# Hi and lo parts of the latent tokens and FFN rows in one tile, and one 512-column matmul of the hi weights with both

## The chip, the cores and the metric

One core of a Trainium2 chip. The metric is the device time of one execution in microseconds: before, the median of three runs is 1982.09 us (1978.47 to 1982.77).

## What is computed

One layer of a hybrid backbone on a latent stream `x` and a context stream `ctx` of 256 tokens each, with 2048 features:

```
px = modulate(rms_norm(x, norm_mix), sh1, sc1) @ w_in          # and pc, from ctx
yx = concat(rwkv(px), short_conv(px), fourier(px)) @ w_out     # the scans of x start from ctx's last states
x  = x + ga1 * yx
h  = modulate(rms_norm(x, norm_ffn), sh2, sc2)
x  = x + ga2 * ((silu(h @ w_gate) * (h @ w_up)) @ w_down)      # 5632 hidden features
out = rms_norm(x, norm_final)
```

All weights and inputs are float32.

## The kernel before

Features lie on the 128 partitions, so 2048 features are 16 **K-tiles**, and the 256 tokens are the columns that a matmul streams. The large products are made in three matmuls of a faster type (`float32r`): a value is split into a hi part, its rounding to that type, and a lo part, the rest. A K-tile of `w^T x` is then hi weights times hi tokens, hi weights times lo tokens, and lo weights times hi tokens, all added in one PSUM bank:

```python
    def mm3(self, out, wh, wl, xh, xl, start, stop):
        self.mm(out, wh, xh, start, False)
        self.mm(out, wh, xl, False, False)
        self.mm(out, wl, xh, False, stop)
```

Every call of `mm` (line 233, so the trace shows line 233 for all matmuls) is a load of 128 x 128 weights and a matmul of 256 columns. `wblock` (L271) brings weights: a DMA from SP's queue into `w`, a cast to `whi` (L266), and a subtraction into `wlo` (L269); each of the three has three places. `XH1` and `XL1` are the hi and lo parts of the latent tokens, `XH0` and `XL0` those of the context.

The stages, in the order of time:
- **Phase A and keys** (to about 280 us): norms, modulation vectors, first projections, for both streams (`mm6`, six matmuls a K-tile).
- **The recurrence** (to about 1150 us): chunked scans of eight pairs of heads for both streams. PE's order is written by hand (`manual_schedule`): between the small matmuls of the scans stand "filling products", a K-tile or a few at a time (`fillers`, `project_steps`). Those of the values take both streams; 26 blocks of 128 columns take the latent alone: 8 queries (`query`), 2 gates, 12 of the short convolution, 4 of the Fourier mixing. Their bank is read by `conv3`, by copies or by multiplications. Then come the products with `w_out` (`out_proj`).
- **SwiGLU, gate and up** (1180 to 1717 us): 44 rows of 128 hidden features. A row has four blocks of weights of 8 K-tiles each (gate, up, gate, up), and two banks, `gu0` and `gu1`. The first two rows go side by side before the norm's factor is known; the 42 others run one after another. ACT takes silu of `gu0` (L1165), DVE multiplies by `gu1` (L1166), and the row is split into `HH` and `HL`. In four rows `modvec` (L1082) brings 16 pieces of `wmb` through two places on SP's queue and adds them up on DVE (L1093).
- **SwiGLU, down** (1717 to 1965 us): 16 blocks of 128 output features, each 44 K-tiles in six blocks of weights (the last one half as long) into a bank `dn`, which DVE scales and adds to `X1` (L1183); then the final norm.

In the SwiGLU stage the casts to `whi` are ACT's, and of the subtractions every third is POOL's and the others DVE's. On all engines but PE in the recurrence a scheduler sets the order when the program is built, from a timeline of its own.

Of the kernel before, what the change touches and what calls it, by code (L numbers as in the profile page):

```python
# [10 lines left out]
F32 = mybir.dt.float32  # L11
F32R = mybir.dt.float32r
# [5 lines left out]
P = 128  # L18
D = 2048
KT = D // P  # L20
L = 256
# [37 lines left out]
class Cols:  # L59
    """Column map of a packed [128, n] array."""  # L60
# [140 lines left out]
class Builder:  # L201
# [12 lines left out]
    def wide(self, dt):  # L214
        """The place with room for two more columns a K-tile."""
        return self.t(self.cp, [P, KT, L + 2], dt, "XH0")
# [19 lines left out]
    def pull(self):  # L236
        """One piece of the filling products; its share of the tensor engine in us."""
        c = next(self.fill, None)
        return 0.0 if c is None else c
# [8 lines left out]

    def mm3(self, out, wh, wl, xh, xl, start, stop):
        self.mm(out, wh, xh, start, False)  # L250
        self.mm(out, wh, xl, False, False)
        self.mm(out, wl, xh, False, stop)

    def mm6(self, out, wh, wl, k, streams=(0, 1)):
        """One K-tile of w^T x for the streams side by side in one bank: only the bank's first
        matmul starts it, the other stream's first one finds its columns cleared."""
# [14 lines left out]
    def wblock(self, src, n, g, pool, tag="w32", bufs=None):  # L271
        """Loads n K-tiles of a 128-column weight block and splits them into hi and lo."""
# [8 lines left out]
    def headsel(self, p, slot):  # L281
        """[16, 128] selector of the two heads of pair p."""
# [5 lines left out]
    def rsqrt(self, out, v, tmp):  # L288
        """out = 1/sqrt(v); one Newton step on top of sqrt and reciprocal."""
# [7 lines left out]
    def rms_add(self, ps, sq, k):  # L297
        """Adds K-tile k to the sums of squares, each quarter of the tokens in its own column tile."""
# [4 lines left out]
    def rms_finish(self, sums, pool, pspool, n, tag, scaled=False):  # L303
        """1/sqrt(mean square + eps) of n tokens, broadcast over the partitions in PSUM."""
# [15 lines left out]
    def conv3(self, out, ps, taps, groups, glen):  # L320
        """out[t] = w0 ps[t-1] + w1 ps[t] + w2 ps[t+1], zero outside each group."""
# [10 lines left out]
    def build(self, stop_after=None):  # L332
        tc, nc, a = self.tc, self.nc, self.a
        with ExitStack() as base:
# [6 lines left out]
            # hi and lo parts of the normalised tokens, context and latent  # L341
            self.XH = [self.wide(F32R)[:, :, :L], self.t(cp, [P, KT, L], F32R, "XH1")]
            self.XL = [self.t(cp, [P, KT, L], F32R, f"XL{s}") for s in range(2)]
# [3 lines left out]
            with ExitStack() as kvs:  # L347
# [5 lines left out]
                # rows past the 96 of the LoRA: the norms of the keys and selectors of heads  # L353
                self.rn = self.wdT[HN]
                self.wend = self.t(kv, [P, NP, 2, C], F32, "wend")
                # keys of the context, two pairs a tile: their places later take the latent's "mq"
# [25 lines left out]
    def small_prep(self, pa):  # L382
        """Derived per-feature scalars and the masks of the block inverse."""
# [27 lines left out]
    def phase_a(self, st):  # L411
# [9 lines left out]
        # silu(c) as zero-padded stationaries  # L421
# [6 lines left out]
        # rms statistics of both streams  # L428
# [49 lines left out]
        # the banks of the last two blocks are needed first  # L478
# [24 lines left out]
    def project_steps(self, blk, streams):  # L503
        ps = self.t(self.pj, [P, 2 * L], F32, "pj")
        for g in range(KT // G4):
            h, lo = self.wblock(self.a["wib"][blk, :, G4 * g:G4 * g + G4], G4, G4, self.wst)
            for j in range(G4):
                self.mm6(ps, h[:, j], lo[:, j], G4 * g + j, streams)
                yield MM3 * len(streams)
        return ps  # L510

# [22 lines left out]
    def value(self, p):  # L534
        # places: three of their own, then in turn those and the used-up keys of the context
# [10 lines left out]
    def query(self, p):  # L546
        pj = yield from self.project_steps(self.blk_r + p, (1,))
        self.conv3(self.Y[:, p], pj[:, :L], self.vec("sh_rkv", 3 * p, 3), 1, L)
        self.queried = p + 1

# [4 lines left out]
    def rw_prep(self, st):  # L555
        """Scaled keys and queries, Gram blocks, values token-major."""
# [9 lines left out]
        # normalised keys, and [kk | k] mixed over the two heads  # L566
# [9 lines left out]
        # decay and in-context rate  # L576
# [9 lines left out]
        # values, token-major: [U; V] of the even head, [V; U] of the odd head  # L586
# [39 lines left out]
        for d in range(2):  # L626
            # Gram blocks
# [15 lines left out]
        # token-major copies of the scaled keys  # L643
# [8 lines left out]
        # minus the intra-chunk part of the values  # L652
# [8 lines left out]
        if s:  # L661
            # bonus: (sum_j r (kf + kb) r_k) v
# [13 lines left out]
    def rw_decay(self, st, d, pl):  # L676
        """Tanh parts of direction d; returns what traces its running products of the decay."""
# [31 lines left out]
    def rw_inverse(self, st, d):  # L709
        """T = (I + M)^-1 of direction d: merges of blocks by two, then a Newton step in float32."""  # L710
# [55 lines left out]
    def rw_scan(self, st):  # L766
        """The state over the chunks, both directions side by side; st["W"]: the state before each step."""
# [8 lines left out]
        for i in range(NC):  # L776
            cc = (i, NC - 1 - i)
            # chunk cc[0] of the first direction and cc[1] of the second among the 2 * NC chunks
# [52 lines left out]
    def rw_out(self, st, Ws):  # L831
        """y of the latent stream, centred per head, and its squares."""
# [15 lines left out]
        # the keys of this pair are used up: their place takes the squares  # L848
# [3 lines left out]
    def recurrence(self):  # L852
        """Both streams of all pairs, a step of each running part at a time, the filling products between."""
# [5 lines left out]
        # block-diagonal over the two heads; the zeros stay  # L859
# [43 lines left out]
    def fillers(self):  # L903
        """Gate, short-convolution and Fourier projections, a block at a time."""
# [4 lines left out]
        def proj():  # L909
# [3 lines left out]
            return ps[:, :L]  # L913
# [298 lines left out]
```

## Time and profile before

| | us |
|---|---|
| median of 3 runs | 1982.09 |
| lowest, highest run | 1978.47, 1982.77 |
| span of the profiled execution | 1980.6 |
| PE, DVE, ACT, POOL busy in it | 1848.4, 1100.7, 831.1, 800.0 |
| chain that ended last: PE's part of the span | 47% |

The profiled execution has no time of its own in the list of runs: its span, from the first to the last instruction, is 1.5 us below the median. PE's busy time is modelled (matmuls overlap one another in it), so the gap from one matmul's start to the next tells more than its duration. "Idle before" in the profile is the time for which an engine stood still ahead of an instruction, with what ended it.

### The profile page before, as it was taken

To read this page: it belongs to the slowest core of one execution; us is meant where nothing else is said; L and a number is where in the kernel's file an instruction comes from. 1 tells how busy PE (TensorE), PEld (TensorE's weight loads), DVE (VectorE), ACT (ScalarE), POOL (GpSimd) and SP (SyncE) were. 2 spreads that over 40 slices of the span, in tenths; PEclk is the share of its full clock that TensorE was granted. 3 is DMA by queue.
4 is the path that set the end of the run, shared out by engine and by line. 5 is a ranking of instruction groups with operands and counts; after the bars stand their busy time and mean duration, and the time that the engine had idled before them with its cause. 6 is when DMAs were issued, how large, how long until landed. Compare 5 with 4: busy or idle time off the path is not lost.

```text
span 1980.6 us, 44697 instructions
## 1 busy us (share of the span) xinstructions
PE 1848.4 (93%) x18488; PEld 1679.4 (85%) x18488; DVE 1100.7 (56%) x1883; ACT 831.1 (42%) x1657; POOL 800.0 (40%) x718
## 2 busy tenths in 40 slices
PE   7888999999999999899999888999999999999997
PEld 4777898888888887687887678999999899999997
DVE  4445257777678766656666378546454543332333
ACT  2213365555555554434443144343434344444442
POOL 1214455466577644535554144222222222223222
PEclk9999999999899988889898689999999999999998
DMA  8883223444444442343433025767676755556564
GB/s 326 292 269 122 78 84 120 139 140 150 133 157 150 132 125 90 104 141 109 115 113 110 24 85 157 247 194 250 194 234 192 225 181 182 184 188 191 185 194 133
DMA packets 139228, 318.75 MB, mean 161 GB/s; under 512 B 14224, under 2 KB 40464, under 8 KB 139024
## 3 DMA queue, kind: packets, MB, share of 16 engines
q1 hardware_dynamic: 137936, 314.84, 50.1%
q8 instruction: 145, 2.38, 0.5%
q10 hardware_dynamic: 1088, 1.05, 0.2%
q14 instruction: 59, 0.48, 0.1%
HBM read 313.74 MB, written 2.10 MB: 159 GB/s over the span
## 4 chain that ended last, share of the span: by engine, by line
PE 47%; DVE 8%; DMA 4%; ACT 1%; issue 1%; POOL 0%; DVEq 0%; SPq 0%; ACTq 0%; POOLq 0%
PE gu L233 20%; PE dn L233 12%; PE acc L233 5%; PE pj L233 5%; DMA XH<-wmb 3%; PE iv L233 2%; PE st L233 1%; PE pp L233 1%; DVE macc L1064 1%; DVE XH L1093 1%; DVE XL L1150 1%; DVE wlo L269 1%; DVE eb L730 0%; ACT whi L266 0%; DVE xn L1148 0%
## 5 line engine op out<-in xcount | busy, mean ns | idle before, releaser
L269 POOL TENSOR_TENSOR wlo<-w,whi 128x512 fp32r<-128x512 f32 (+2 forms) x309 | 518.8, 1682 | 783.4 <-ACT whi L266 746.8
L266 ACT CAST whi<-w 128x1024 fp32r<-128x1024 f32 (+2 forms) x472 | 400.7, 849 | 576.1 <-PE gu L233 192.9
L233 PE MATMUL gu<-XH,wlo 128*128 128x256 f32 (+1 forms) x1408 | 402.5, 286 | 13.0 <-DVE wlo L269 9.1
L233 PE MATMUL gu<-XH,whi 128*128 128x256 f32 (+1 forms) x1408 | 401.5, 285 | 4.1 <-ACT whi L266 4.0
L233 PE MATMUL gu<-XL,whi 128*128 128x256 f32 x1344 | 381.3, 284 | 0.0
L269 DVE TENSOR_TENSOR wlo<-w,whi 128x1024 fp32r<-128x1024 f32 (+1 forms) x175 | 208.3, 1191 | 301.9 <-ACT whi L266 295.3
L233 PE MATMUL pj<-XH,whi 128*128 128x256 f32 x1016 | 291.5, 315 | 2.9 <-DVE XL L998 1.3
L233 PEld LDWEIGHTS gu<-XH,wlo 128*128 128x128 f32 x1408 | 269.6, 192 | 15.7 <-DVE wlo L269 11.0
L233 PEld LDWEIGHTS gu<-XH,whi 128*128 128x128 f32 x1408 | 269.7, 192 | 5.1 <-ACT whi L266 4.8
L233 PE MATMUL pj<-XL,whi 128*128 128x256 f32 x1016 | 262.5, 287 | 0.6 <-DVE XL L269 0.6
L233 PE MATMUL pj<-XH,wlo 128*128 128x256 f32 x1016 | 262.3, 287 | 0.0
L233 PEld LDWEIGHTS gu<-XL,whi 128*128 128x128 f32 x1344 | 256.0, 190 | 0.2 <-DVE XL L1150 0.2
L233 PEld LDWEIGHTS pj<-XH,whi 128*128 128x128 f32 x1016 | 186.8, 196 | 14.2 <-issue 3.1
L233 PE MATMUL dn<-HL,whi 128*128 128x256 f32 x704 | 196.0, 278 | 0.0
L233 PE MATMUL dn<-HH,wlo 128*128 128x256 f32 x704 | 194.7, 277 | 0.0
L233 PE MATMUL dn<-HH,whi 128*128 128x256 f32 x704 | 194.4, 276 | 0.0
L233 PEld LDWEIGHTS pj<-XL,whi 128*128 128x128 f32 x1016 | 187.2, 196 | 2.5 <-issue 0.9
L233 PEld LDWEIGHTS pj<-XH,wlo 128*128 128x128 f32 x1016 | 186.2, 196 | 2.6 <-POOL whi L268 1.7
L1064 DVE SCALAR_TENSOR_TENSOR macc<-wm,sc,macc 128x512 f32<-128x512 f32 x180 | 170.8, 949 | 4.5 <-DMA wm<-wmb 3.7
L233 PEld LDWEIGHTS dn<-HL,whi 128*128 128x128 f32 x704 | 132.2, 188 | 1.4
L233 PEld LDWEIGHTS dn<-HH,wlo 128*128 128x128 f32 x704 | 132.2, 188 | 0.3 <-POOL wlo L269 0.2
L233 PEld LDWEIGHTS dn<-HH,whi 128*128 128x128 f32 x704 | 132.1, 188 | 0.0
(312 smaller groups left out, 3027.4 us busy)
## 6 DMA issues: line engine op xcount, KB each, us to landing
w<-wgu SPq DMA_DIRECT2D x176, 512.0 KB, 4.5
wm<-wmb SPq DMA_DIRECT2D x192, 256.0 KB, 3.0
w<-wdn SPq DMA_DIRECT2D x80, 512.0 KB, 4.5
w<-wib SPq DMA_DIRECT2D x148, 256.0 KB, 3.2
wm<-wma SPq DMA_DIRECT2D x64, 512.0 KB, 7.7
XH<-wmb SPq DMA_DIRECT2D x64, 256.0 KB, 4.1
w<-wout SPq DMA_DIRECT2D x48, 256.0 KB, 3.2
wa<-wia SPq DMA_DIRECT2D x16, 416.0 KB, 8.8
```

Of the source, the lines that this page charges most:

```text
L233: self.last = self.nc.tensor.matmul(out, lhsT=lhsT, rhs=rhs, start=start, stop=stop)
L266: he.copy(hi, src)
L269: le.tensor_tensor(lo, src, hi.bitcast(F32), op=ALU.subtract)
L1064: V.scalar_tensor_tensor(acc, w, self.sc[:, k, 1:2], acc, op0=ALU.mult, op1=ALU.add)
L1093: nc.vector.scalar_tensor_tensor(acc, w, self.sc[:, k, 1:2], acc, op0=ALU.mult, op1=ALU.add)
L1150: V.scalar_tensor_tensor(XL[:, k], xn, bias, XH[:, k].bitcast(F32), op0=ALU.add, op1=ALU.subtract)
```

## The change

The hi and lo parts of the latent tokens become two halves of one tile `XP`, those of the hidden rows two halves of `HX`. A K-tile is then two matmuls: the hi weights with both halves side by side (512 columns, a whole bank), and the lo weights with the hi half (256 columns, the bank's first half). The sum of the bank's halves is made afterwards: `both` copies the second half to SBUF on ACT and adds the first on DVE; in the down product, DVE adds the halves to `X1` one after the other. It is done for the 26 single-stream projections, the 42 rows of gate and up, and the down product; `mm6`, `out_proj` and the first two rows keep their form.

```diff
+    def mm3w(self, out, wh, wl, k, xs, start, stop):
+        self.mm(out, wh, xs[:, :, k], start, False)
+        self.mm(out[:, :L], wl, xs[:, 0, k], False, stop)
...
-            self.XH = [self.wide(F32R)[:, :, :L], self.t(cp, [P, KT, L], F32R, "XH1")]
-            self.XL = [self.t(cp, [P, KT, L], F32R, f"XL{s}") for s in range(2)]
+            self.XP = self.t(cp, [P, 2, KT, L], F32R, "XP")
+            self.XH = [self.wide(F32R)[:, :, :L], self.XP[:, 0]]
+            self.XL = [self.t(cp, [P, KT, L], F32R, "XL0"), self.XP[:, 1]]
...
-                self.mm6(ps, h[:, j], lo[:, j], G4 * g + j, streams)
+                k = G4 * g + j
+                if len(streams) == 2:
+                    self.mm6(ps, h[:, j], lo[:, j], k, streams)
+                else:
+                    self.mm3w(ps, h[:, j], lo[:, j], k, self.XP, k == 0, k == KT - 1)
...
+    def both(self, out, ps):
+        self.nc.scalar.copy(out, ps[:, L:])
+        self.nc.vector.tensor_tensor(out, out, ps[:, :L], op=ALU.add)
+        return out
...
-        self.conv3(self.Y[:, p], pj[:, :L], self.vec("sh_rkv", 3 * p, 3), 1, L)
+        self.conv3(self.Y[:, p], self.both(self.ar[:, p % 8], pj), self.vec("sh_rkv", 3 * p, 3), 1, L)
...
+        def plain():
+            return self.both(ar[:, blk % 8], (yield from proj()))
...
-            self.conv3(self.sg[:, j], (yield from proj()), self.vec("sh_gd", 3 * j, 3), 1, L)
+            self.conv3(self.sg[:, j], (yield from plain()), self.vec("sh_gd", 3 * j, 3), 1, L)
...
-            S.copy(cg, (yield from proj()))
-            V.tensor_tensor(cg, cg, (yield from proj()), op=ALU.mult)
+            self.both(cg, (yield from proj()))
+            V.tensor_tensor(cg, cg, (yield from plain()), op=ALU.mult)
...
-            S.copy(u, (yield from proj()))
+            self.both(u, (yield from proj()))
...
-        HH = T(fp, [P, NFF, L], F32R, "HH", 1)
-        HL = T(fp, [P, NFF, L], F32R, "HL", 1)
+        HX = T(fp, [P, 2, NFF, L], F32R, "HX", 1)
+        HH, HL = HX[:, 0], HX[:, 1]
...
-                            self.mm3(pgu[2 * i + w], h[:, j], lo[:, j], xh[:, k], xl[:, k], k == 0, k == KT - 1)
+                            if xh is None:
+                                self.mm3w(pgu[2 * i + w], h[:, j], lo[:, j], k, self.XP, k == 0, k == KT - 1)
+                            else:
+                                self.mm3(pgu[2 * i + w], h[:, j], lo[:, j], xh[:, k], xl[:, k], k == 0, k == KT - 1)
...
-                pgu = gate_up((f,), XH, XL)
-                S.activation(sg, pgu[0], AF.Silu)
-                vi = V.tensor_tensor(sg, sg, pgu[1], op=ALU.mult)
+                pg, pu = gate_up((f,))
+                self.both(sg, pg)
+                S.activation(sg, sg, AF.Silu)
+                su = self.both(T(fp, [P, L], F32, "xn"), pu)
+                vi = V.tensor_tensor(sg, sg, su, op=ALU.mult)
...
-            pd = T(fps, [P, L], F32, "dn")
+            pd = T(fps, [P, 2 * L], F32, "dn")
...
-                    self.mm3(pd, h[:, j], lo[:, j], HH[:, f], HL[:, f], f == 0, f == NFF - 1)
-            V.scalar_tensor_tensor(X1[:, m], pd, self.mod[:, 3, m:m + 1], X1[:, m], op0=ALU.mult, op1=ALU.add)
+                    self.mm(pd, h[:, j], HX[:, :, f], f == 0, False)
+                    self.mm(pd[:, :L], lo[:, j], HH[:, f], False, f == NFF - 1)
+            for i in range(2):
+                V.scalar_tensor_tensor(X1[:, m], pd[:, L * i:L * i + L], self.mod[:, 3, m:m + 1], X1[:, m],
+                                       op0=ALU.mult, op1=ALU.add)
```

PE's order in a row of gate and up, before (two K-tiles; `XH` and `XL` are `XH1` and `XL1`):

```order
L233 MATMUL gu_2994_18897<-XH_2631_15881,whi_18989 128x256
L233 MATMUL gu_2994_18897<-XL_2632_15882,whi_18989 128x256
L233 MATMUL gu_2994_18897<-XH_2631_15881,wlo_18990 128x256
L233 MATMUL gu_2994_18897<-XH_2631_15881,whi_18989 128x256
L233 MATMUL gu_2994_18897<-XL_2632_15882,whi_18989 128x256
L233 MATMUL gu_2994_18897<-XH_2631_15881,wlo_18990 128x256
```

and now (three K-tiles):

```order
L233 MATMUL gu_3040_18184<-XP_62,whi_18187 128x512
L233 MATMUL gu_3040_18184<-XP_62,wlo_18188 128x256
L233 MATMUL gu_3040_18184<-XP_62,whi_18187 128x512
L233 MATMUL gu_3040_18184<-XP_62,wlo_18188 128x256
L233 MATMUL gu_3040_18184<-XP_62,whi_18187 128x512
L233 MATMUL gu_3040_18184<-XP_62,wlo_18188 128x256
```

Two matmuls, and so two loads, stand where three did.

ACT's order around the end of a row of gate and up, before (`sg` is the row, `gu_3145` its bank `gu0`):

```order
L266 CAST whi_20340<-w_3162_20339 128x1024
L266 CAST whi_20370<-w_3165_20369 128x1024
L1165 ACTIVATE sg_20209<-gu_3145_20210 128x256
L266 CAST whi_20400<-w_3168_20399 128x1024
L266 CAST HH_15883<-sg_20209 128x256
L266 CAST whi_20430<-w_3171_20429 128x1024
```

and now (`gu_3152` and `gu_3153` are the row's `gu0` and `gu1`):

```order
L271 CAST whi_19025<-w_3171_19024 128x1024
L271 CAST whi_19047<-w_3174_19046 128x1024
L524 COPY sg_18915<-gu_3152_18916 128x256
L271 CAST whi_19069<-w_3177_19068 128x1024
L524 COPY xn_19009<-gu_3153_18917 128x256
L1188 ACTIVATE sg_18915<-sg_18915 128x256
L271 CAST whi_19091<-w_3180_19090 128x1024
L271 CAST HX_15506<-sg_18915 128x256
```

Two copies are new, and the silu reads SBUF; the second copy, which waits for the end of `gu1`, stands behind the cast of the third block of the next row.

SP's queue in the first `modvec` (`XH_2683` there is the place of its pieces), before:

```order
L1089 DMA XH_2683_16224<-wmb 128x2x256 x2
L276 DMA w_2741_16693<-wgu 128x1024
L276 DMA w_2744_16723<-wgu 128x1024
L1089 DMA XH_2683_16224<-wmb 128x2x256 x2
L276 DMA w_2747_16753<-wgu 128x1024
L1089 DMA XH_2683_16224<-wmb 128x2x256
L276 DMA w_2753_16790<-wgu 128x1024
L1089 DMA XH_2683_16224<-wmb 128x2x256
```

and now:

```order
L1107 DMA XH_2677_15846<-wmb 128x2x256 x2
L281 DMA w_2741_16248<-wgu 128x1024
L1107 DMA XH_2677_15846<-wmb 128x2x256 x2
L281 DMA w_2744_16270<-wgu 128x1024
L1107 DMA XH_2677_15846<-wmb 128x2x256
L281 DMA w_2751_16304<-wgu 128x1024
L1107 DMA XH_2677_15846<-wmb 128x2x256
```

But for one block of weights that now comes ahead of the first pieces, the pattern is the same.

## Rows read from the trace of the kernel before

**Rows 1.** The page: busy time of engines, and the chain that ended last.
```profile
PE 1848.4 (93%) x18488; PEld 1679.4 (85%) x18488; DVE 1100.7 (56%) x1883; ACT 831.1 (42%) x1657; POOL 800.0 (40%) x718
...
PE gu L233 20%; PE dn L233 12%; PE acc L233 5%; PE pj L233 5%; DMA XH<-wmb 3%; PE iv L233 2%; PE st L233 1%; PE pp L233 1%; DVE macc L1064 1%; DVE XH L1093 1%; DVE XL L1150 1%; DVE wlo L269 1%; DVE eb L730 0%; ACT whi L266 0%; DVE xn L1148 
```

**Rows 2.** Busy time of engines (instructions), granted clock, DMA, by stretch of SwiGLU.
```profile
1219.00:1239.00 20.00, 19.94 (x161) 19.50 (x161) 11.71 (x18) 9.50 (x15) 4.80 (x2) 0.97 0.51 158
1239.00:1279.00 40.00, 37.75 (x314) 37.14 (x313) 23.68 (x30) 15.10 (x20) 10.85 (x4) 1.00 0.76 257
1279.00:1334.00 55.00, 55.00 (x466) 55.00 (x466) 22.44 (x26) 23.24 (x30) 14.38 (x6) 1.00 0.63 198
1334.00:1375.00 41.00, 38.59 (x321) 37.98 (x320) 28.27 (x30) 14.84 (x20) 13.34 (x5) 1.00 0.82 261
1375.00:1427.00 52.00, 52.00 (x441) 52.00 (x440) 20.66 (x23) 22.59 (x28) 14.36 (x6) 1.00 0.61 189
1427.00:1466.00 39.00, 34.68 (x267) 34.27 (x266) 22.32 (x29) 13.13 (x16) 8.22 (x4) 0.91 0.75 235
1466.00:1540.00 74.00, 74.00 (x626) 74.00 (x625) 34.27 (x36) 30.78 (x39) 21.50 (x9) 1.00 0.63 202
1540.00:1580.00 40.00, 35.49 (x282) 34.91 (x281) 22.52 (x27) 13.76 (x18) 10.53 (x4) 0.96 0.74 234
1580.00:1717.00 137.00, 137.00 (x1157) 137.00 (x1156) 56.52 (x57) 57.45 (x72) 38.33 (x16) 1.00 0.60 184
1717.00:1969.00 252.00, 248.27 (x2249) 244.36 (x2249) 83.22 (x103) 100.64 (x113) 74.37 (x31) 1.00 0.56 178
```

**Rows 3.** Waits, 1219 to 1969 us: who waited for whom, us, times, longest.
```profile
ACT whi L266 <- PE gu L233: 192.9, 116, 2.6
...
ACT whi L266 <- DMA w<-wgu: 79.1, 35, 5.1
DVE XH L1093 <- DMA XH<-wmb: 60.5, 38, 4.7
...
ACT whi L266 <- DMA w<-wdn: 37.3, 23, 3.0
```

**Rows 4.** PE in order of time (start, duration), first and last of 25 in `gu`.
```profile
1500.04 0.28 PE L233 MATMUL gu<-XH,whi 128*128 128x256 f32 x1
...
1502.89 0.28 PE L233 MATMUL gu<-XH,whi 128*128 128x256 f32 x1
```

**Rows 5.** The same view, first and last of 37 in `dn`.
```profile
1847.86 0.28 PE L233 MATMUL dn<-HH,whi 128*128 128x256 f32 x1
...
1851.94 0.28 PE L233 MATMUL dn<-HH,whi 128*128 128x256 f32 x1
```

**Rows 6.** The same view, PE's loads (PEld): one alone, and eight with `macc`.
```profile
342.21 0.19 PEld L233 LDWEIGHTS pj<-XH,wlo 128*128 128x128 f32 x1
342.34 0.98 PEld L233 LDWEIGHTS pj<-consts,macc 128*128 128x128 f32 x8
```

**Rows 7.** Plain f32 passes: time order (256, 512 columns), duration of one (256, 512).
```profile
662.19 0.60 PE L233 MATMUL pp<-adT,lora 96*128 96x256 f32 x2
...
L233 PE MATMUL pp<-adT,lora x2: 379/380/380, 662.2 to 662.4; 96*128 96x256 f32 x2
...
199.50 1.88 PE L233 MATMUL acc<-bkt,consts 128*16 128x512 f32 x4
...
L233 PE MATMUL acc<-bkt,consts 128*16 128x512 f32 x8 | 3.6, 593 | 0.0
```

**Rows 8.** Instructions of tile `XL`, 380 to 1150 us: duration in ns, min/median/max.
```profile
L929 ACT COPY XL<-pj x4: 360/364/367, 550.2 to 676.3; 128x256 f32<-128x256 f32 x4
L930 DVE TENSOR_TENSOR XL<-XL,pj x4: 404/413/420, 563.4 to 694.3; 128x256 f32<-128x256 f32 x4
```

**Rows 9.** POOL in `dn`, in order of time [idle before <- what ended it].
```profile
1853.88 2.40 POOL L269 TENSOR_TENSOR wlo<-w,whi 128x1024 fp32r<-128x1024 f32 x1 [5.89 <-ACT whi L266]
1861.01 2.39 POOL L269 TENSOR_TENSOR wlo<-w,whi 128x1024 fp32r<-128x1024 f32 x1 [4.73 <-ACT whi L266]
```

More of the change, by code (lines that the diff above doesn't have):

```diff
@@ L912, in proj @@
             ps = yield from self.project_steps(blk - 1, (1,))
-            return ps[:, :L]
+            return ps
+        def plain():
+            return self.both(ar[:, blk % 8], (yield from proj()))
         for p in range(2, NP):
@@ L917, in fillers @@
         self.Y = self.wide(F32)[:, :, :L]
-        ar = T(self.cp, [P, KT, L], F32, "XL0")
+        ar = self.ar = T(self.cp, [P, KT, L], F32, "XL0")
         self.sg = T(self.mp, [P, 2, L], F32, "sg")
@@ L928, in fillers @@
             cg, cv = ar[:, 12], ar[:, 13]
-            S.copy(cg, (yield from proj()))
-            V.tensor_tensor(cg, cg, (yield from proj()), op=ALU.mult)
+            self.both(cg, (yield from proj()))
+            V.tensor_tensor(cg, cg, (yield from plain()), op=ALU.mult)
             self.conv3(cv, cg, self.vec("conv_w", 3 * j, 3), 4, 64)
-            V.tensor_tensor(self.Y[:, 8 + j], cv, (yield from proj()), op=ALU.mult)
+            V.tensor_tensor(self.Y[:, 8 + j], cv, (yield from plain()), op=ALU.mult)
         cds = ar[:, 13]
@@ L991, in out_proj @@
         nc, V, G, T = self.nc, self.nc.vector, self.nc.gpsimd, self.t
-        YH = T(self.cp, [P, KT, L], F32R, "XH1")
-        YL = T(self.cp, [P, KT, L], F32R, "XL1")
+        YH, YL = self.XP[:, 0], self.XP[:, 1]
         self.X1 = T(self.cp, [P, KT, L], F32, "XL0")
@@ L1108, in phase_ffn @@
         X1 = self.X1
-        XH = T(self.cp, [P, KT, L], F32R, "XH1")
-        XL = T(self.cp, [P, KT, L], F32R, "XL1")
+        XH, XL = self.XP[:, 0], self.XP[:, 1]
         self.modps, self.modtag = fps, "st"
-        HH = T(fp, [P, NFF, L], F32R, "HH", 1)
-        HL = T(fp, [P, NFF, L], F32R, "HL", 1)
+        HX = T(fp, [P, 2, NFF, L], F32R, "HX", 1)
+        HH, HL = HX[:, 0], HX[:, 1]
         uh = self.uh
@@ L1125, in phase_ffn, with gate_up @@
         self.leng = lambda n: nc.gpsimd if n <= 10 or n % 3 == 0 else nc.vector
-        def gate_up(fs, xh, xl, norm=None):
-            pgu = [T(fps, [P, 2 * L], F32, f"gu{w}")[:, :xh.shape[2]] for _ in fs for w in range(2)]
+        def gate_up(fs, xh=None, xl=None, norm=None):
+            pgu = [T(fps, [P, 2 * L], F32, f"gu{w}") for _ in fs for w in range(2)]
+            if xh is not None:
+                pgu = [pg[:, :xh.shape[2]] for pg in pgu]
             for g in range(0, KT, G8):
```

## The prediction, made before the changed kernel was run

> **What bounds the kernel now.** I read the busy shares and the chain that ended last first [rows 1]: TensorE (PE) is busy 93% of the span, and the two largest pieces of the chain, 20% and 12% of the span, are its `gu` (the gate and up products) and `dn` (the down products). PE's busy time is modelled, so I then took the SwiGLU stage apart into stretches [rows 2]. Five of them (1219 to 1239, 1279 to 1334, 1375 to 1427, 1466 to 1540, 1580 to 1717) have PE busy throughout; together they are 338 us with 161 + 466 + 441 + 626 + 1157 = 2851 matmuls, 118.6 ns each. The four between them (1239, 1334, 1427, 1540 to their ends) are 160 us with only 314 + 321 + 267 + 282 = 1184, 135 ns each: there `modvec` brings 16 pieces of `wmb` through two places, VectorE (DVE) waits for them [rows 3], and its splits of weights into `wlo` stand behind in its queue. In two of these PE's clock also fell for a while (PEclk 0.91 and 0.96), after PE had paused.
>
> What does PE do in a full stretch? The matmuls in time order: in `gu` 24 gaps between 1500.04 and 1502.89, or 118.8 ns each [rows 4]; in `dn` 36 gaps from 1847.86 to 1851.94, or 113.3 ns, very even [rows 5]. The granted clock is 1.00 there [rows 2], 2.4 GHz, at which 256 columns are 106.7 ns, so columns alone fill neither. Next, what a weight load costs by itself: eight matmuls of only two columns against `macc` [rows 6]. Their eight loads take 0.98 us, the last one's own 0.19 included (the row above it shows one alone), so (0.98 - 0.19) / 7 = 113 ns from load to load with next to nothing to stream. That is the gap of `dn`. My reading: each matmul brings its own load of 128 columns of weights, which runs beside the matmul before it, and at 256 columns the load (113) is longer than the stream (107). **The load sets the pace.** PE then waits for almost nobody, and ScalarE (ACT), which makes `whi`, mostly waits for PE to free its place: 192.9 us in `gu`, against 79.1 us for DMAs [rows 3].
>
> **What a K-tile costs after the change.** Before: three loads, three matmuls of 256 columns. After: two loads, one matmul of 512 and one of 256. The load of `wlo` now hides behind 512 columns, and only the load of the next `whi` is longer than what covers it. No fp32r matmul of 512 columns is in this trace, so its price is bounded by its neighbours. Plain f32 passes: two of 256 columns take 0.60 us in all where one takes 0.38, so 0.22 apart [rows 7], twice the time of the fp32r stream; four of 512 columns, a full bank, take 1.88 with 593 ns for one, so (1.88 - 0.593) / 3 = 0.43 apart [rows 7]. So a pass is linear in its columns, and a full bank has no surcharge. Half of 0.43 is 0.215: I take **216 ns** for the new matmul. Below, 512 / 2.4 = 213 is the floor; above, twice a gap of today (227 in `dn`, 238 in `gu`) is what it costs if the gap follows the columns and not the load, and the f32 price of 430 is the far end.
> - `dn`: 3 x 113.3 = 340 becomes 216 + 113 = 329: **10.7 ns** a K-tile. There are 16 x 44 = 704: 7.5 us.
> - `gu` outside the four stretches: 3 x 118.8 = 356 becomes 216 + 119 = 335: **21 ns**. 2851 / 3 = 950 K-tiles: 20.0 us. The trace does not say why `gu` is 5.5 ns slower a matmul. I take it for the load (it is what sets the pace) and leave it in the last term; with 113 there, it would be 27 ns, and if the columns are what is slow, nothing.
> - `gu` in the four stretches: the time is that of the 16 DMAs, two places, and DVE. The queue of SP issues them in the same pattern as before, one block of weights after each piece or two. A faster PE waits there longer: **0 us**. Bounds: all 394 K-tiles gain too (8.3 us less), or one or two more drops of PE's clock cost 3 to 7 us.
> - Single-stream projections in the recurrence, 26 blocks of 16: 416 K-tiles at 11 ns, the price of `dn`, 4.5 us of PE time, of which perhaps half lies on the path.
> - `both`, added there: 26 copies on ACT of 0.364 us and 26 additions on DVE of 0.413 us [rows 8], 9.5 and 10.7 us. The queries run several pairs ahead of the latent's scan, and the copy lets go of the bank sooner than the three steps of the convolution did, so most of it is covered by the recurrence's other work. Uncovered are the four Fourier blocks, where PE's own next product waits for the sum: 4 x 0.5 = 2 us. Bounds: none of it, or 20 us if every step stood on the path. With the 4.5 us above I put the recurrence at **0**.
> - `both` in SwiGLU: two copies and two additions a row more, 0.73 us on ACT and 0.83 on DVE. In the last full stretch, 12 rows of them, ACT is busy 57.5 of 137 us and DVE 56.5 [rows 2], so 9 or 10 us more on each leave both under half full. The copy of `gu1` comes in ACT's queue behind the cast that waits for the same end of the row on PE, so no cast is later for it: free.
> - The second addition of `dn`: taken at the 0.41 us of the addition above, hidden behind the next block but for the last: **+0.4 us** at the very end.
>
> **Does the supply keep up?** The place of a weight block goes round in DMA, cast and split; every third block has its split on POOL, 2.4 us. The fastest round that I see in `dn` goes from the end of one such split to the end of the next in the same place, 1853.88 + 2.40 = 1856.28 to 1863.40 [rows 9], 7.1 us, with the DMA and the cast between. Three blocks of `gu` need 3 x 8 x 0.335 = 8.0 us: covered by 0.9. In `dn` an output block of 44 K-tiles is then 14.5 us and holds two such rounds, 14.2 to 14.5: **covered by little**. If the change gained more in `dn`, this is what would be late next.
>
> The sum: -20.0 - 7.5 + 0 + 0 + 0.4 = -27.1 us against the span of 1980.6, or 1953.5. The median of the three runs, 1982.1, stands 1.5 above the span, so I forecast **1955 us**.
>
> A rule that speaks against the change: the Trainium skill, "TensorE: Matmul & The Clock Gate", section "Back-to-back issue gap", puts the warm gap of a matmul by itself at N / 2.4 + 2.5 ns, 109 at 256 columns and 216 at 512 (with loads between, it says, both count). Were that all, a K-tile would lose 2.5 ns, 6 us over the kernel. The trace disagrees at 256 columns, with 113 and 119, and agrees with the 216.
>
> **The rivals.**
> - *More* (0.12): all of `gu` at 113, 27 ns, and the four stretches follow too, 1344 x 27 = 36, with `dn` and some of the recurrence: -45 us, 1937. For it: `dn` shows the same load at 113. Against: the DMA chain in the stretches is not touched.
> - *The supply becomes the bound* (0.13): POOL's round holds `gu` at 2.77 us a block in place of 2.68 and `dn` at half its gain: 119 blocks x 0.08 = 9.5, and 3.7: -13 us, 1969. For it: ACT already waits for DMAs 35 times in `gu`, 23 times in `dn` [rows 3]. Against: PE never stops outside the stretches.
> - *Columns, not loads* (0.10): the 512 columns cost twice 256 less a fixed 2 ns, as in f32, where 2 x 0.216 is 0.43. 2464 K-tiles x 2 ns: -5 us, or 1977 to 1982 as the additions cost a little. For it: `gu` is slower than a load alone.
> - *The wide matmul is dearer than its columns* (0.07): it reads its two halves 16 KB apart (44 KB in `dn`) and fills its bank. Place: each changed K-tile. It decides from 238 ns in `gu` and 227 in `dn`; at 250 it costs 950 x 12 + 704 x 23 = 28 us and the kernel is at 2010. Against: the f32 rows with 512 columns pay nothing for the full bank; for it: no fp32r row with two halves is in the trace.
> - That the change does not do what it says is excluded: PE's order has the two matmuls.
>
> **The numbers.** Forecast 0.58, more 0.12, supply 0.13, columns 0.10, dearer 0.07. A difference of 0.2%, 4 us, is about what a measurement of this kernel can tell from none. Faster: the first three and a third of columns, 0.86; no difference: 0.07; slower: 0.07. The range leaves out the dearer case and most of columns: 1937 (more) to 1975 (supply, with 6 us for a clock drop or additions on the path).
>
> **What would show it.** Right: in `gu` the gaps alternate, about 216 after `whi` and 113 to 119 after `wlo`; 1580 to 1717 shrinks by some 6%; the 704 K-tiles of `dn`, 340 ns each, come down to 329; the four stretches keep their 40 us and hold more PE waits on `wlo`; the recurrence ends within 5 us of where it did. Wrong: a gap after `whi` of 230 or more (columns), waits of PE on POOL's `wlo` in the full stretches (supply), or PEclk under 0.9 in more than two stretches.

## The result, and the profile after

Median of 15 runs of each: **1993.8 us** after (1983.8 to 2003.6), 1982.3 us before (1973.3 to 1992.0). The ratio is **1.0055, 95% interval 1.0036 to 1.0075**: slower by 11 us, where 27 us less were forecast. The profiled execution took 1990.4 us, its span is 1988.6, 8.0 above that of before.

The page of the changed kernel, busy time and chain:

```profile
PE 1845.6 (93%) x16024; PEld 1549.5 (78%) x16024; DVE 1207.0 (61%) x2009; ACT 860.8 (43%) x1759; POOL 797.3 (40%) x718
...
PE gu L233 16%; PE dn L233 13%; DMA XH<-wmb 5%; PE acc L233 4%; PE pj L233 4%; PE iv L233 2%; PE st L233 1%; DVE XH L1111 1%; PE pp L233 1%; DVE wlo L274 1%; DVE XP L1172 1%; DVE macc L1082 1%; DVE HX L1138 1%; ACT whi L271 0%; DVE eb L746 0%
```

Against [rows 1], 2464 matmuls and as many loads are gone, and 130 us of load time with them; PE's busy time is what it was. So the loads are gone, and no time went with them. The last full stretch of gate and up and the down projection, by stretch:

```profile
1580.00:1717.00 137.00, 137.00 (x778) 118.74 (x777) 72.53 (x82) 65.32 (x98) 38.59 (x17) 1.00 0.58 187
1717.00:1977.00 260.00, 256.13 (x1540) 218.68 (x1538) 119.49 (x120) 99.68 (x115) 74.53 (x31) 1.00 0.56 172
```

At the same granted clock and with PE never idle, 137 us hold 778 / 2 = 389 K-tiles; before they held 1157 / 3 = 386 [rows 2]. That is 1% more where 6% was forecast. The down projection takes some 8 us more. The matmuls in time order show why, in `gu`:

```profile
1501.15 0.28 PE L233 MATMUL gu<-XP,wlo 128*128 128x256 f32 x1
1501.27 0.40 PE L233 MATMUL gu<-XP,whi 128*128 128x512 f32 x1
1501.51 0.28 PE L233 MATMUL gu<-XP,wlo 128*128 128x256 f32 x1
1501.62 0.40 PE L233 MATMUL gu<-XP,whi 128*128 128x512 f32 x1
1501.85 0.28 PE L233 MATMUL gu<-XP,wlo 128*128 128x256 f32 x1
```

and in `dn`, the first four and the last of a stretch:

```profile
1847.63 0.40 PE L233 MATMUL dn<-HX,whi 128*128 128x512 f32 x1
1847.87 0.28 PE L233 MATMUL dn<-HX,wlo 128*128 128x256 f32 x1
1847.99 0.40 PE L233 MATMUL dn<-HX,whi 128*128 128x512 f32 x1
1848.22 0.28 PE L233 MATMUL dn<-HX,wlo 128*128 128x256 f32 x1
...
1851.88 0.40 PE L233 MATMUL dn<-HX,whi 128*128 128x512 f32 x1
```

From a `whi` start (the wide matmul, 512 columns) to the next `wlo` start (a narrow one, 256 columns) is 230 to 240 ns, from there to the next `whi` 110 to 120. In `dn` 12 K-tiles lie between 1847.63 and 1851.88: (1851.88 - 1847.63) / 12 = **354 ns** a K-tile, 340 before [rows 5], 329 forecast. In `gu` the last stretch gives 137 us / 389 = 352 ns, before 137 / 386 = 355, forecast 335. By the first matmul of each stage in the two traces, the recurrence ends 4.4 us later (1173.4 to 1177.8), gate and up last 4.8 us less (544.4 to 539.6), the down projection 8.3 us more (246.8 to 255.1): +7.9 of the 8.0.

The waits of SwiGLU, 1219 to 1977 us:

```profile
ACT whi L271 <- PE gu L233: 130.3, 95, 1.8
...
ACT whi L271 <- DMA w<-wgu: 55.2, 31, 3.9
DVE XH L1111 <- DMA XH<-wmb: 49.3, 34, 2.9
...
ACT whi L271 <- DMA w<-wdn: 30.9, 17, 2.1
```

Each of these DMA waits is shorter than before [rows 3]: the supply did not become the bound.

### The profile page after: what moved, and what is told of

The parts are those of the page before. It is cut to its first block, busy times and chain, and to the rows that moved or that the text cites. A ratio compares the mean times of both kernels' runs of the same rounds, so it can differ in the third digit from the quotient of the medians.

```text
span 1988.6 us, 39977 instructions
## 1 busy us (share of the span) xinstructions
PE 1845.6 (93%) x16024; PEld 1549.5 (78%) x16024; DVE 1207.0 (61%) x2009; ACT 860.8 (43%) x1759; POOL 797.3 (40%) x718
## 4 chain that ended last, share of the span: by engine, by line
PE 41%; DVE 9%; DMA 5%; issue 1%; ACT 1%; POOL 0%; DVEq 0%; SPq 0%; ACTq 0%; POOLq 0%
PE gu L233 16%; PE dn L233 13%; DMA XH<-wmb 5%; PE acc L233 4%; PE pj L233 4%; PE iv L233 2%; PE st L233 1%; DVE XH L1111 1%; PE pp L233 1%; DVE wlo L274 1%; DVE XP L1172 1%; DVE macc L1082 1%; DVE HX L1138 1%; ACT whi L271 0%; DVE eb L746 0%
## 5 line engine op out<-in xcount | busy, mean ns | idle before, releaser
L233 PE MATMUL gu<-XP,whi 128*128 128x512 f32 x1344 | 476.5, 399 | 3.4 <-ACT whi L271 2.6
L233 PE MATMUL gu<-XP,wlo 128*128 128x256 f32 x1344 | 380.6, 283 | 14.0 <-DVE wlo L274 11.6
L233 PE MATMUL pj<-XP,whi 128*128 128x256 f32 (+1 forms) x1264 | 371.8, 347 | 2.7 <-DVE XL L1016 2.1
L233 PEld LDWEIGHTS gu<-XP,whi 128*128 128x128 f32 x1344 | 253.6, 189 | 64.7 <-ACT whi L271 3.0
L233 PEld LDWEIGHTS gu<-XP,wlo 128*128 128x128 f32 x1344 | 255.3, 190 | 19.5 <-DVE wlo L274 15.9
L233 PEld LDWEIGHTS pj<-XP,whi 128*128 128x128 f32 x1264 | 230.5, 197 | 26.4 <-issue 2.5
L233 PE MATMUL dn<-HX,whi 128*128 128x512 f32 x704 | 249.3, 397 | 0.0
L233 PE MATMUL pj<-XP,wlo 128*128 128x256 f32 x840 | 242.5, 289 | 0.0
L233 PE MATMUL dn<-HX,wlo 128*128 128x256 f32 x704 | 199.4, 283 | 0.0
L233 PEld LDWEIGHTS pj<-XP,wlo 128*128 128x128 f32 x840 | 166.1, 198 | 0.5
```

Of the source, the lines that this page charges most:

```text
L233: self.last = self.nc.tensor.matmul(out, lhsT=lhsT, rhs=rhs, start=start, stop=stop)
```

## The experiments

**1. Is it the gap between the halves?** The changed kernel with the two halves of a K-tile next to each other, so that the wide matmul reads 512 columns in one piece.

```diff
-            self.XP = self.t(cp, [P, 2, KT, L], F32R, "XP")
+            self.XP = self.t(cp, [P, KT, 2, L], F32R, "XP")
...
-        HX = T(fp, [P, 2, NFF, L], F32R, "HX", 1)
+        HX = T(fp, [P, NFF, 2, L], F32R, "HX", 1)
```

> The change with hi and lo of one K-tile side by side in memory, so that the 512 columns are one contiguous piece. Theory A (the two halves far apart, 16 KB and 44 KB, are what makes the wide matmul slow): the gap after whi falls from 233-235 ns to 216, a K-tile of dn from 353 to about 330 ns and of gu from 350 to about 334; time about 1955 us, 2% below the change. Theory B (a float32r stream is paced by its columns, about 0.46 ns each, whatever the layout): gaps stay at 233-235 and the time at about 1994 us. Theory C (traffic of the other engines and DMAs slows PE's reads): as B.

Measured: ratio to before 1.0067 (1.0042 to 1.0092), no better than the change itself. In `dn`:

```profile
1847.77 0.40 PE L233 MATMUL dn<-HX,whi 128*128 128x512 f32 x1
1848.01 0.28 PE L233 MATMUL dn<-HX,wlo 128*128 128x256 f32 x1
1848.13 0.40 PE L233 MATMUL dn<-HX,whi 128*128 128x512 f32 x1
1848.36 0.28 PE L233 MATMUL dn<-HX,wlo 128*128 128x256 f32 x1
```

Again 230 to 240 and 120, and 353 ns a K-tile. The two pieces cost nothing; theory A falls.

**2 to 4. PE alone, then beside DMAs, then beside the other engines.** A small kernel with nothing but the matmuls on ready data.

```diff
+            def trip(name, reps=1):
+                        self.mm(o[:, :L], h[:, k % 8], XP[:, 0, k], s, False)
+                        self.mm(o[:, :L], h[:, k % 8], XP[:, 1, k], False, False)
+                        self.mm(o[:, :L], lo[:, k % 8], XP[:, 0, k], False, e)
+            def gapped(name, reps=1):
+                        self.mm(o, h[:, k % 8], XP[:, :, k], s, False)
+                        self.mm(o[:, :L], lo[:, k % 8], XP[:, 0, k], False, e)
+            def cols(name, c, off=0, m=32):
+                    self.mm(o[:, :c], (h, lo)[i % 2][:, i % 8], f[:, off + 256 * (i % 16):off + 256 * (i % 16) + c],
+                            i == 0, i == m - 1)
```

> PE alone, no other engine or DMA at work: the K-tile before (trip), the K-tile of the change (gapped), the same with the halves adjoining (joined), then loads with 64 to 512 contiguous columns, and 256 and 512 columns starting 32 bytes further on. All of the layer's computation is left out; the output is a copy of the input. Theory A: joined 216 after whi, gapped 235. Theory B: both 235, c512 235, c256 118, a line of 0.46 ns a column down to the load's 112 ns. Theory C: gapped and joined both 216, trip 109-113. If the load sets the pace of 256 columns, c64 to c256 are all 112-113 ns.

> trip, gapped and joined of the last kernel, four times as long, while 30 DMAs of 512 KB run on SP's queue and no other engine works. The layer's computation is left out. Theory A and B: gaps as in the quiet kernel. Theory C, if the DMAs are it: 235 after whi here and 216 in the quiet kernel.

> trip, gapped and joined while ACT casts, and DVE and POOL subtract, 1024 columns at a time in SBUF, without DMAs. The layer's computation is left out. Theory A and B: gaps as in the quiet kernel. Theory C, if the engines are it: 235 after whi here and 216 in the quiet kernel.

PE alone in time order: three narrow matmuls a K-tile (two K-tiles), wide and narrow, and 512 columns each with a load of its own:

```profile
31.12 0.40 PE L24 MATMUL trip<-XP,wh 128*128 128x256 f32 x2
31.36 0.28 PE L24 MATMUL trip<-XP,wl 128*128 128x256 f32 x1
31.48 0.40 PE L24 MATMUL trip<-XP,wh 128*128 128x256 f32 x2
...
36.16 0.40 PE L24 MATMUL gapped<-XP,wh 128*128 128x512 f32 x1
36.40 0.28 PE L24 MATMUL gapped<-XP,wl 128*128 128x256 f32 x1
36.52 0.40 PE L24 MATMUL gapped<-XP,wh 128*128 128x512 f32 x1
...
53.83 0.39 PE L24 MATMUL c<-XP,wh 128*128 128x512 f32 x1
54.06 0.39 PE L24 MATMUL c<-XP,wl 128*128 128x512 f32 x1
54.28 0.39 PE L24 MATMUL c<-XP,wh 128*128 128x512 f32 x1
```

The three narrow ones take 360 ns, the wide pair 354 (236 and 118, medians), 512 columns with a load each 227. Theory C, traffic, asked for 216 after `whi` with PE alone, so it falls here. Beside the other engines and DMAs it was 120, 235 to 236 and 117 to 118 again. In these two runs the narrow matmuls had all of that traffic beside them; the wide pair had the DMAs for its first 10 of 22 us, DVE throughout, POOL for half, and ACT not at all. By columns, with a load for each matmul, the median gaps were 112 ns (64 columns), 111 to 113 (128), 110 to 113 (192), 120 (256), 147 (320), 173 (384), 227 (512). Up to 192 columns the gap does not change with the columns: the load sets it. Above, a gap is the columns at 2.4 GHz and **some 13 ns more**: 133.3 + 13.7, 160 + 13, 213.3 + 13.7. So theory B holds in kind, with a fixed piece for each matmul, of which the forecast allowed 2.7 ns. A full bank costs no more than a part of one (13.7 against 13 to 13.7). Two variants began 32 bytes further on: 512 columns took 234 ns there, and 256 took 117 (213 in the part where, after 10 us of 192 to 64 columns a load, the granted clock was down at 1.2 GHz; its mean from 80 to 85 us was 0.72): a first sign that place matters. The fixed piece does not explain `dn` before, where 256 columns took 113 and not 120.

**5. What sets the piece?** PE alone, 19 variants of 48 or 32 matmuls: tokens or weights shifted, other banks, the same K-tile again, a higher place.

```diff
+    dict(bank=2), dict(bank=2, so=8), dict(bank=2, so=16), dict(bank=2, so=24),
+    dict(bank=3, wo=8), dict(bank=3, wo=16), dict(bank=3, wo=24),
+    dict(bank=4, so=8, wo=8), dict(bank=4, so=24, wo=8),
+    dict(bank=5, do=256), dict(bank=6), dict(bank=7), dict(bank=7, same=True),
+    dict(bank=6, X="Y"), dict(bank=6, X="Y", so=24, wo=8),
+    dict(bank=2, wide=True), dict(bank=3, wide=True, so=8, wo=8), dict(bank=4, wide=True, so=24, wo=8),
+    dict(bank=5, wide=True, X="Y")
```

> TensorE alone, nothing else of the program is computed: 48 matmuls each of three 256-column float32r matmuls a K-tile (h with hi, h with lo, lo with hi) or of one 512-column and one 256-column, with the tokens moved by 0, 32, 64 or 96 bytes, the weights by 0, 32, 64 or 96 bytes, the sum in another bank or in a bank's second half, the same K-tile again and again, or the tokens 56 KB further up. The earlier measurement fits a matmul's gap as its columns at 2.4 GHz plus a fixed piece of 6.7, 13.3 or 20 ns, with the load's 112 ns as floor. Theory B1 (the fixed piece hangs on where tokens or weights lie): gaps of 113 at some offsets and 120 at others; down projection's combination (tokens +96, weights +32) 113, gate and up's (tokens +32, weights +32) 119. Theory B2 (it hangs on the bank or half): 113 in banks 6 and 7, 120 in the others. Theory B3 (it hangs on neither, the kernel's own order or data set it): 120 for every three-matmul variant, 236 and 118 for every wide one.

Time order, one row a variant (`so`, `wo`: columns of 4 bytes by which tokens and weights are shifted); in this order: no shift, `so=16`, `wo=8`, `so=8 wo=8`, `so=24 wo=8`, other half of a bank, bank 6, and `Y` with `so=24 wo=8`:

```profile
35.02 5.92 PE L32 MATMUL b<-X,W 128*128 128x256 f32 x48
...
46.54 5.64 PE L32 MATMUL b<-X,W 128*128 128x256 f32 x48
...
57.80 5.56 PE L32 MATMUL b<-X,W 128*128 128x256 f32 x45
...
74.88 5.62 PE L32 MATMUL b<-X,W 128*128 128x256 f32 x46
...
80.58 5.40 PE L32 MATMUL b<-X,W 128*128 128x256 f32 x46
85.93 5.74 PE L32 MATMUL b<-X,W 128*128 128x256 f32 x47
91.62 5.74 PE L32 MATMUL b<-X,W 128*128 128x256 f32 x47
...
114.45 5.70 PE L32 MATMUL b<-Y,W 128*128 128x256 f32 x47
```

A gap is (time - 0.28) over the matmuls less one. No shift 5.64 / 47 = 120.0 ns; `so=16` 5.36 / 47 = **114.0**; `so=8 wo=8` 5.34 / 45 = 118.7; `so=24 wo=8` 5.12 / 45 = **113.8**; the other half and bank 6 5.46 / 46 = 118.7. So banks and halves move the gap by 1.3 ns at most (120.0 in bank 2, 118.7 in banks 5 to 7, at one place), and place by 6: B1, whose 113 and 119 for the combinations of the two stages came out as 113.8 and 118.7, but in a way that needed sorting. `Y` with the same shifts as the 113.8 gives 5.42 / 46 = 117.8, because `Y` itself begins elsewhere. What orders all rows is the place of tokens minus that of weights in a partition, in bytes, modulo 256 (worked out from the sizes of the program's tiles; a trace shows no addresses):

```
difference        0      32     64     96     128          160    192           224
gap, ns           119.5  117.8  117.8  120.0  118.7-120.0  117.4  113.8, 114.0  118.2
```

Only 192 comes down to the 113 of the load. In the kernel before, the difference is 192 in the down projection (113.3) and 128 in gate and up (118.8): both agree to 0.7 ns with the rows above, but for the 120.0 at 128. Modulo 128 would not do, since 64 is slow. The wide pair took 350 to 353 ns a K-tile at 128 and 192, 354 at 0 in run 2: nothing fast at any difference.

**6 and 7. The parts apart.** The change with the down projection put back; and the kernel before with gate and up alone changed, but with the tokens' joint tile first, as in the change (both edits are shown against the changed kernel; run 7 has the edit of run 6 too, and `both` is taken out wherever the recurrence used it).

```diff
-                    self.mm(pd, h[:, j], HX[:, :, f], f == 0, False)
-                    self.mm(pd[:, :L], lo[:, j], HH[:, f], False, f == NFF - 1)
+                    self.mm3(pd, h[:, j], lo[:, j], HH[:, f], HL[:, f], f == 0, f == NFF - 1)
```
```diff
-                if len(streams) == 2:
-                    self.mm6(ps, h[:, j], lo[:, j], k, streams)
-                else:
-                    self.mm3w(ps, h[:, j], lo[:, j], k, self.XP, k == 0, k == KT - 1)
+                self.mm6(ps, h[:, j], lo[:, j], G4 * g + j, streams)
...
-            self.both(u, (yield from proj()))
+            S.copy(u, (yield from proj()))
```

> The changed kernel with the down projection put back to three 256-column matmuls and one product into the sum. If the wide form itself costs the down projection its pace: gaps of 113 again there, the stage from 255 back to 247 us, total about 8 us below the changed kernel, ratio to before about 1.0015 (1.000 to 1.003). If something else of the change (the addresses, the joint tile of hi and lo rows) slowed it: gaps of 118 remain, stage about 249 to 255 us, ratio 1.003 to 1.006.

> The kernel before with the wide matmul in gate and up alone; projections of the recurrence and down projection as before. If the three parts of the difference add up (recurrence +4.4, gate and up -4.7, down projection +8.4): gate and up's stage 539 to 540 us, recurrence ends as before, the down projection at 113 a matmul, ratio 0.9976 (0.996 to 0.999), faster than both. If gate and up's 4.7 us were chance or came from the recurrence's shift: ratio 1.000. If the vector engine's new adds beside the loads cost something there: 1.001 to 1.003.

Down projection back: ratio **1.000** (0.9977 to 1.0023). Its stage is 246.2 us again, and its K-tiles take 340 ns:

```profile
1715.00:1950.00 235.00, 235.00 (x2135) 231.72 (x2134) 77.52 (x92) 95.88 (x107) 74.34 (x31) 1.00 0.59 186
```

(235 / 2135 = 110 ns with the sums of squares counted in, as before.) Gate and up alone: **0.994** (0.9915 to 0.9964), 1966.8 us, faster than both kernels and more than the 0.9976 expected: in its profile gate and up take 530.5 us, not 539 to 540, and the recurrence ends 5.7 us earlier than before. So the wide form cost the down projection its 0.5%, the recurrence's part costs 0.6% (1979.9 against 1966.8 us, 13 us), and the rest of the change, gate and up with the place of the tokens, gains 0.6% (12 us).

**8 and 9. Only the place.** The kernel before, narrow matmuls everywhere, with 192 bytes that nobody uses ahead of the FFN rows (shown), or behind them (the same line after `HL`).

```diff
+        S.copy(T(fp, [P, 48], F32, "pad", 1)[:, :1], self.ones32[:, :1])
         HH = T(fp, [P, NFF, L], F32R, "HH", 1)
         HL = T(fp, [P, NFF, L], F32R, "HL", 1)
```

> The kernel before with 192 unused bytes ahead of the FFN rows, which move the rows and the SwiGLU's weight blocks up together and nothing else. Taken modulo 256, tokens minus weights is then 192 in gate and up (128 before) and still 192 in the down projection. If that difference sets the pace, as the TensorE-alone run had it (341.8 ns a K-tile at 192, 356.2 at 128): gate and up from 356 to 342 a K-tile, the down projection stays at 340, gate and up's stage 13 to 19 us shorter, ratio 0.990 to 0.9935. If the agreement was chance: 356 stays and the ratio is 1.000.

> The kernel before with the same 192 bytes behind the FFN rows: only the SwiGLU's weight blocks move. The difference becomes 192 in gate and up and 0 in the down projection. If it sets the pace: gate and up at 342 a K-tile as in the run with the bytes ahead, the down projection from 340 to 356 to 360 (TensorE alone 356 to 360 at 0), so its stage about 12 to 14 us longer, and the sum near nothing: ratio 0.996 to 1.000. If it does not: neither stage moves, ratio 1.000, gaps 356 and 340.

Ahead: ratio 0.996 (0.9929 to 0.9991). Behind: 0.9992 (0.997 to 1.0013). By stretch, `gu` at its end and `dn`; first before,

```profile
1580.00:1700.00 120.00, 120.00 (x1014) 120.00 (x1013) 50.90 (x51) 50.29 (x63) 33.55 (x14) 1.00 0.59 183
1720.00:1960.00 240.00, 240.00 (x2174) 236.42 (x2173) 79.13 (x94) 97.33 (x108) 74.37 (x31) 1.00 0.58 184
```

then `gu` with the bytes ahead,

```profile
1580.00:1700.00 120.00, 120.00 (x1061) 120.00 (x1061) 52.20 (x51) 52.82 (x67) 35.20 (x15) 1.00 0.62 196
```

then with them behind:

```profile
1580.00:1700.00 120.00, 120.00 (x1021) 120.00 (x1020) 51.39 (x51) 50.55 (x64) 33.51 (x14) 1.00 0.59 186
1720.00:1960.00 240.00, 240.00 (x2069) 236.63 (x2068) 74.15 (x90) 92.75 (x104) 69.80 (x30) 1.00 0.56 175
```

The same stretch of before holds 1014 matmuls (120 / 1014 = 118.3 ns); now 1061, 113.1 ns, from a shift of 192 bytes alone. With the bytes behind, `dn` goes to 240 / 2069 = 116 ns with the sums of squares counted in (before 240 / 2174 = 110); its K-tiles go from 340 to **360 ns** and the stage from 246.8 to 259.8 us, +13.0, as expected. Place is a cause, then. Three things did not fit. With the bytes ahead the ratio was 0.996 where 0.990 to 0.9935 was expected; of its twelve executions six took 1962 to 1967 us and five 1979 to 1986, as long as before, and the profiled one is of the first kind. In it gate and up became 12.8 us shorter, just under the 13 to 19 expected: the K-tiles that ran through gave 17 us, and those with a wait in them took back some 5. And `gu` with the bytes behind (its stage 10.9 us shorter) runs at 117.5 at its end at the same difference. The K-tiles counted by length (from one `wlo` matmul to the next, each put down to the nearest of four lengths; the few longer ones left out) show what that is:

```
                       340    347    353    360 ns
before          gu       -      6    764    554
before          dn     658     15     11      -
change          gu       -    655    329    340
change          dn       -      -    673      -
run 7 (gu wide) gu       -   1040    134    148
run 8 (ahead)   gu    1014      2    276     28
run 9 (behind)  gu     803      7    484     23
run 9 (behind)  dn       -      -     16    672
```

An even stream takes 51, 52, 53 or 54 steps of 6.67 ns a K-tile (340.0, 346.7, 353.3, 360.0). The others are uneven with a period, and only the period is a whole number of steps: `gu` before repeats 361, 354, 354, 359, 352 ns, five K-tiles in 1780 ns (267 steps, 356 each); the wide pair repeats 355, 346, 359, three in 1060 ns (159 steps, 353 each), so a third of these stand at 347 in the table. A stream that has fallen into one pattern keeps it, often for tens of us. At difference 192 narrow matmuls run at 51 steps, or at 53 (a fifth of the K-tiles in run 8, over a third in run 9); at 128, in `gu` before, they have the period of five; at 0 they take 54. The wide pair runs evenly at 52 or with the period of three in gate and up (in the change's profile two thirds of the K-tiles have that period, in run 7 a quarter), and at 53 in the down projection.

**10 to 12. What costs the recurrence?** The change with narrow matmuls in the down projection, put back as in run 6, and in the recurrence, where they still fill two halves that are added; gate and up alone changed, plus the copies and additions into rows nobody reads; and gate and up alone changed, with the tokens' tile moved back behind the context's.

```diff
-                    self.mm3w(ps, h[:, j], lo[:, j], k, self.XP, k == 0, k == KT - 1)
+                    xh, xl = self.XP[:, 0, k], self.XP[:, 1, k]
+                    self.mm(ps[:, :L], h[:, j], xh, k == 0, False)
+                    self.mm(ps[:, L:], h[:, j], xl, False, False)
+                    self.mm(ps[:, :L], lo[:, j], xh, False, k == KT - 1)
```
```diff
+    def spare(self, x):
+        t = self.ar[:, self.uses % 8]
+        self.nc.scalar.copy(t, x)
+        self.nc.vector.tensor_tensor(t, t, x, op=ALU.add)
...
+        self.spare(self.Y[:, p])
```
```diff
+            xh0 = self.wide(F32R)[:, :, :L]
             self.XP = self.t(cp, [P, 2, KT, L], F32R, "XP")
-            self.XH = [self.wide(F32R)[:, :, :L], self.XP[:, 0]]
+            self.XH = [xh0, self.XP[:, 0]]
```

> The changed kernel with three 256-column matmuls both in the down projection and in the recurrence's latent projections, which still lay hi*lo into the bank's other half and add the halves behind; the wide matmul is left in gate and up alone. It differs from the run with gate and up changed alone by the adding of halves, and from the run with the down projection put back by the wide matmul of the recurrence. If the adding costs the recurrence its time: ratio 0.999 to 1.002, as in the run with the down projection put back, PE waits on DVE's add as in the changed kernel. If the wide matmul does: ratio 0.993 to 0.996, as with gate and up changed alone.

> The kernel with gate and up changed alone, plus one ACT copy and one DVE add of 256 columns behind each of the 26 latent projections of the recurrence, into rows that nobody reads, from the product already in SBUF: the work of adding halves without its place in the chain (no bank waits for it, no reader does). If the engines' work itself costs the 13 us by which the runs with halves stand above the run with gate and up alone: ratio 0.999 to 1.002. If the place does (the bank is held longer, and the reader comes later): ratio 0.993 to 0.996, with no PE wait on the add.

> The kernel with gate and up changed alone, with the joint tile of latent tokens placed behind the context's hi rows as before, so that tokens minus weights, modulo 256, is 192 again in the recurrence's latent projections (64 with the tile placed first) and 128 in gate and up (0). If the pace of the matmuls bears on the recurrence's end: gaps of latent projections 113 to 116 for 118, ratio 0.990 to 0.994. If the recurrence is set by its chain: 0.994 as with the tile placed first. Gate and up stay at 345 to 351 a K-tile.

Narrow with halves added: 1.0008 (0.9983 to 1.0033), as with the wide matmul there (1.000): so it is the filling and adding of halves that costs; of the wide matmul in the recurrence these intervals show neither gain nor loss. The work alone, off the chain: 0.9974 (0.9948 to 0.9999), between the two theories, its interval touching both; in the profiles its recurrence ends at 1172.0 us, between 1167.7 (run 7) and 1177.2 (run 6). How the cost divides between the work on ACT and DVE and its place in the chain is not settled. Direct waits on the sum exist; the changed kernel, PE's waits from 380 to 1165 us:

```profile
PE iv L233 <- DVE idm L773: 19.3, 10, 3.1
PE st L233 <- DVE w L830: 9.3, 10, 2.0
PE pj L233 <- DVE XL L525: 6.5, 4, 2.6
```

6.5 us for the four Fourier blocks, and 19.3 on `idm` of the block inverse, 15.1 before (on `w` 11.2 before). In run 6 the first two are 6.6 and 20.0, in run 7 none and 14.8, in run 11 none and 15.4: in these traces the waits come with the place in the chain. With the tile moved back: 0.996 (0.994 to 0.998); the gap of the recurrence's projections went from 118 to 114 ns at the median, and the recurrence ended 3 us earlier, but gate and up at difference 128 took 351 ns a K-tile (a period of three in 1053 ns) where run 7 had 347 for most, and 7 us more. No gain over run 7, but a check of it: at the places of before, the wide form in gate and up is still worth 0.4%, so run 7's gain is not all from moving the tokens.

## Why the prediction was wrong

- *The load sets the pace*: this step failed for `gu`. The load takes 111 to 113 ns (run 2 and [rows 6]), and `dn` before, at 113.3, lies at that or just above; no run tells it from 256 columns plus one step of 6.7 ns. I took it for `gu` too and left the 5.5 ns by which `gu` is slower in the load's account. They belong to the place: with the same loads, 256 columns come to 113, 118 or 120 by where tokens lie against weights. Run 8 moved 192 bytes and `gu` ran at 113. What in PE takes longer at the other places stays open. The two gaps, 118.8 and 113.3 [rows 4, 5], at one clock and of one shape, held the warning.
- *216 ns for the wide matmul*: the mis-sized term. It measured 227 with its own kind and 230 to 236 with a narrow one behind, which is the sign of being wrong that the prediction named. I allowed 2.7 ns over the columns, from half of an f32 pass [rows 7]; it is 14 to 22. With 117 for the narrow one a K-tile takes 347 to 354, not 329 and 335. The Trainium skill, "TensorE: Matmul & The Clock Gate", section "Back-to-back issue gap", has the same 216 for a warm matmul by itself (N / 2.4 + 2.5). With a load for each, run 2 measured 227. The prediction says that the trace agrees with the 216; what agreed was half of an f32 pass, and the trace has no float32r matmul of 512 columns.
- *`dn`, -7.5 us*: +8.3. Narrow matmuls ran near the load's pace there, 340 ns a K-tile, and the wide pair's 353 ns does not reach that.
- *`gu`, -20 us*: -4.8 in the profile of the change, about -12 in the medians of run 7, in whose profile it kept the even 347 ns for longer: 9 ns a K-tile in place of 21. In that profile the K-tiles that ran through give 9 us; the rest of its gain lies in shorter waits and in the recurrence.
- *The recurrence, 0 (the additions 0 to +20)*: +4.4 in the profiles, and 13 us between the medians of runs 6 and 7. Inside the bounds; the value was wrong. Waits on the sum in the Fourier blocks were 6.5 us, 2 were allowed.
- *`both` in SwiGLU free, supply sufficient, clock*: right. In the last stretch ACT is busy 65 and DVE 73 of 137 us while PE never stops; PE waited 14.7 us for `wlo` in all of gate and up, 11.3 before. The granted clock is 1.00 in both stretches.
- *The rivals*: "columns, not loads" had the price (twice today's gap, 227 and 238; measured 230 to 236), but forecast 0 to 5 us less, not 11 more. "Dearer than its columns" had the sign and the point from which it decides, 227 in `dn`, which was passed (235); of its two mechanisms, halves apart was refuted by run 1, and the full bank has no sign in run 2. Together they had 0.17, and the forecast 0.58, because an f32 row was taken as the nearest price where the two fp32r gaps of the trace itself were nearer.

The sum as measured: `gu` -12 (run 7, with what moving the tokens did), `dn` +9 (its stage, change against run 6), adding halves in the recurrence +13, or +10 against +11 in the medians; the profiles of single executions give -5, +8, +4. That the two differ by what one execution varies in `gu` and in the recurrence is likely, but not shown.

## What to carry over

Before merging matmuls to save loads, look for two stretches where the same shape runs at two paces: if one already equals the load, the other is held by something else, and that may cost nothing to remove. Here 192 unused bytes gave 0.4% (a mean of executions with the gain and without) where a rewrite of the products lost 0.5%, and the rewrite of gate and up alone gave 0.4 to 0.6%. Take a change apart by stage when its parts meet different paces, and price the work that joins the halves again at the stage with the longest chain.

## What the hardware showed that was not expected

- A float32r matmul of 256 columns with its own load takes 113 to 120 ns by the place of tokens against weights modulo 256 bytes; 192 is the fast one of the eight differences tried (run 5). Why 192, and whether 256 is the period for other tile strides, was not tried.
- Even K-tiles, and the periods of uneven ones, are whole steps of 6.67 ns, the time of 16 columns at 2.4 GHz, and a stream keeps its pattern over many K-tiles. The same gate and up at the same places ran evenly at 347 ns for most of run 7's profile, and with the period of 355, 346, 359 for two thirds of the change's. What chooses the pattern, and what ends it, is open.
